# Filter layers and spectra at later positions, and one pool of twelve weight slots

## The chip, the cores and the metric

The kernel runs on one core of a Trainium2 chip, in one launch. The metric is the device time in microseconds; the figure for a kernel is the median of its runs. All times inside the kernel are from one profiled execution, counted from the start of its span.

## The reference, cut to what matters

Two blocks work on 256 tokens of width 1024, all in fp32. Each has a mixer, a layer norm, a mixture of experts and a layer norm. Block 0's mixer is an attention (with 256 context tokens), block 1's is a Hyena mixer, whose long filters don't depend on the tokens:

```
hid  = sin(sf[0] * (z @ w_in + b[0]))         # z: 256 x 33, constant
hid  = sin(sf[1] * (hid @ w_hid[0] + b[1]))   # 64 wide
hid  = sin(sf[2] * (hid @ w_hid[1] + b[2]))
filt = (hid @ w_out) * decay                  # 256 x 2 x 2 x 1024
spec = rfft(concat(fwd, 0, flip(bwd[1:])))    # per order o and channel
z    = gate * (irfft(rfft(z) * spec[o]) + z * skip[o])      # for o in 0, 1
# mixture of experts, 16 experts of 1024 x 1024 x 3, each token goes to two
ys   = (silu(x @ w_gate[e]) * (x @ w_up[e])) @ w_down[e]
```

Modulation vectors (`c @ mod_w`, 2 x 6 x 1024) scale and shift what goes into the mixers and experts.

## The kernel before, in words

**Stages.** Up to about 265 us: the attention, with the modulation vectors woven between its units. Then the output projection, the router and layer 0's experts (277 to 776), the Hyena mixer (788 to 907), its output projection and router, and layer 1's experts (957 to 1304), then the last layer norm.

**The ring.** All large weights go through tiles of 128 x 2048 fp32 (1 MB each), loaded by SP's queue in the order of the program as the scheduler fixes it (`load`, L146). There are RING = 12 slots, and during the experts of layer l MORE[l] = 4 or 5 further ones in a pool of their own. Before, each slot is a pool tag of its own with one buffer, and `turns` keeps the order in which they come up: a load waits until the one slot whose turn it is has been read out by its last user.

**Experts in positions.** `moe` (L730) takes an expert at a position p. Each needs 8 tiles for gate and up (L648), then 4 for down (L667); the tokens are picked by a one-hot matmul (`pick`, L616), turned (L628), and added back to `xs` (`back`, L686, L692). Positions 0 to 9 are always run. The two fullest experts are done densely for all tokens beside positions 1 to 8 (`PIECES`): at odd positions half of gate and up with 4 more tiles (`dense_up`, L711, L713), at even ones half of down with 2 more (`dense_down`, L723). So an odd position loads 16 tiles and an even one 14.

Positions 10 to 13 are rare: nested branches (`rare`, L761) run an expert only where tokens are left for it. In this data three run in layer 0 and none in layer 1 (108 loads each of gate, up and down tiles, four to an expert, are 27 experts: 12 in each layer and three). The branch is taken at position 9 (NEST), ahead of that position's own expert. Before the branch the queue loads 8 of position 9's tiles; inside it the rare experts use the other slots; after it come the 4 down tiles. What is loaded into a slot that the branch uses waits until TensorE has left the branch.

**Filters.** Layer 0's experts have a filler: `filler(p, bank)` is called at each position after the dense piece and ahead of `turn_in` and `down`. At position 0 it runs `filt_mlp` (loads on POOL's queue, then three layers, each a matmul L1172, six DVE steps L1174 to L1180, and a Sin on ScalarE L1182, each waiting for the one before) and the first two of eight spectra (`filt_spec`: matmuls L1212 and L1221, DVE steps L1213 and L1224, a store to DRAM L1225). FILL names the position of each spectrum. `spec_loads` for the next one (L1195 to L1200, on POOL's queue, one buffer) follows each.

**Hyena mixer.** Its input weights come as two raw tiles per section s of six; in sections 1 to 5 ScalarE and DVE split each into a high and a low part (L154, L155), which takes four more slots (`win_loads`). The spectra are read back into two slots per order (`spec_load`). NAHEAD = 4 raw tiles are asked for at the end of layer 0's experts.

Of the kernel before, what the change touches and what calls it, by code (L numbers as in the profile page):

```python
# [7 lines left out]
F32 = mybir.dt.float32  # L8
# [3 lines left out]
AF = mybir.ActivationFunctionType  # L12
# [14 lines left out]
RING = 12  # L27
# [10 lines left out]

PIECES = {1 + i: (i // 4, i // 2 % 2, i % 2) for i in range(4 * DENSE)}

FILL = [0, 0, 4, 6, 8, 8, 9, 9]

MODS = (12, 34)
MLAG = 2
# [31 lines left out]
def emit(tc, I, O):  # L76
# [3 lines left out]

    with es:
        cp = es.enter_context(tc.tile_pool(name="cp", bufs=1))
        ring = es.enter_context(tc.tile_pool(name="ring", bufs=1))
        accp = es.enter_context(tc.tile_pool(name="accp", bufs=1, space=PSUM))
        miscp = es.enter_context(tc.tile_pool(name="miscp", bufs=1, space=PSUM))
        dram = es.enter_context(tc.tile_pool(name="dram", bufs=1, space=DRAM))
# [15 lines left out]
                mturn[0] ^= 1  # L102
            return miscp.tile([128, 512], F32, name=f"mis{i}", tag=f"mis{i}")

        slots = {"order": list(range(RING)), "at": 0}

        def wtile(i=None):

            if i is None:
                i = turns()[0]  # L110
                slots["at"] += 1
            return (ring if i < RING else slots["pool"]).tile([128, 2048], F32, name=f"w{i}", tag=f"w{i}")

        def turns(order=None):

            if order is None:
                a = slots["at"] % len(slots["order"])
                return slots["order"][a:] + slots["order"][:a]
            slots["order"], slots["at"] = order, 0

        def more_ring(l):

# [4 lines left out]
            return xp, pool_  # L127

        def all_slots(n):
            turns(turns() + [RING + i for i in range(n)])  # L130

        def less_ring(pool_):
            turns([i for i in turns() if i < RING])
            for p_ in pool_:
                p_.__exit__(None, None, None)

# [437 lines left out]
        def expert_loads(l, idx, have=(), most=12, new=False):  # L574

            def src(nm, i):
                return expert_of(l, nm, idx)[256 * i:256 * i + 256, :].rearrange("(k p) f -> p k f", p=128)

            order = [(nm, i) for i in range(4) for nm in ("exp_w_gate", "exp_w_up")] + [("exp_w_down", i) for i in range(4)]
            ts = list(have)  # L580
            for nm, i in order[len(ts):]:
                ts.append(load(src(nm, i), [2, 1024], slot=RING + len(ts) if new else None))
                if len(ts) == most:
                    break
            return ts
# [144 lines left out]
        def moe(l, h2, R, first, filler):  # L730
            with tc.tile_pool(name=f"mp{l}", bufs=2, reuse_waits="tile") as mp:
# [73 lines left out]
                for p in range(RARE):  # L805
                    if p == NEST:

                        ix = number(1, place(p), [ET.SP], NE - 1)
                        w = expert_loads(l, ix, most=8)
                        last.back()  # L810
                        last = None
                        free = turns()
                        own, free = free[-8:], free[:-8]
                        turns(free)
                        rare(RARE)
                        E.bank = E.banks()
                        free.sort(key=lambda i: i < RING)
                        turns(free[:4])
                        E.w = expert_loads(l, ix, have=w)
                        turns(free[4:] + own + free[:4])  # L820
                    elif p == 0:
                        E.w = first
                    else:
                        ix = number(1, place(p), [ET.SP], NE - 1) if p > 1 else 1
                        E.w = expert_loads(l, ix, have=second if p == 1 else (), most=8)
                        if p in PIECES:
                            r, half, down = PIECES[p]
                            dw = dense_loads(l, number(1, 2 + r, [ET.SP], NE - 1), half, down)
                        E.w = expert_loads(l, ix, have=E.w)
                    E.up()  # L830
                    if last:
                        last.back()
                    nxt = expert(p + 1) if p + 1 < RARE else None
                    if nxt:
                        nxt.pick()
                    if p == 0:
                        for t in range(2):
                            dve.tensor_tensor(out=xs[:, t, :], in0=h2[:, t, :], in1=lng, op=ALU.mult)
                            for hf in range(2):
                                s_ = slice(512 * hf, 512 * hf + 512)  # L840
                                dve.tensor_tensor(out=xs[:, t, s_], in0=xs[:, t, s_], in1=lnb[hf], op=ALU.add)
                    E.turn_mid()
                    if p in PIECES:
                        if down:
                            dense_down(mp, E.bank, dw, hid[r], R["wtP"][:, :, 2 + r:3 + r], g2b)
                        else:
                            hid[r] = dense_up(mp, E.bank, dw, h2T)
                    if filler:
                        filler(p, E.bank)
                    if nxt:  # L850
                        nxt.turn_in()
                    if p != NEST:
                        E.weights_in()
                    E.down()
                    if p + 1 == NEST:
                        nxt.weights_in()
                    E, last = nxt, E
# [290 lines left out]
        spec = dram.tile([2, 4, 128, D], F32, name="spec")  # L1148
        fl_state = {}

        def filt_mlp():
            hft = fp.tile([128, 4, FQ], F32, name="hft", tag="stg")
            hfi = hft[0:33, 0, 0:64]
            pool.dma_start(out=hfi, in_=I["hy_ffn_w_in"][0])
            hfh = hft[0:64, 1, 0:128].rearrange("k (a m) -> k a m", a=2)
            pool.dma_start(out=hfh, in_=I["hy_ffn_w_hid"][0].rearrange("a k m -> k a m"))
            hfb = fp.tile([64, 6], F32, name="hfb")
            pool.dma_start(out=hfb[:, 0:3], in_=I["hy_ffn_b"][0].rearrange("a k -> k a"))
            pool.dma_start(out=hfb[:, 3:6], in_=I["hy_sin_freq"][0].rearrange("a k -> k a"))
            mt = fp.tile([128, 4, N], F32, name="mt", tag="PM")  # L1160
            zT = mt[0:33, 0]
            pool.dma_start(out=zT, in_=I["cst_z"])
            fl_state["FF"] = FF = fp.tile([128, 4, 128], F32, name="FF")
            pool.dma_start(out=FF, in_=I["cst_fw"].rearrange("p (c f) -> p c f", c=4))

            hs = fp.tile([128, 2, N], F32, name="hs")
            hid = zT
            kdim = 33
            for a in range(3):
                b = mbank()  # L1170
                w = hfi if a == 0 else hfh[:, a - 1, :]
                pe.matmul(b[0:64, 0:N], w, hid[0:kdim, :], start=True, stop=True)  # L1172
                u, k = mt[0:64, 1], mt[0:64, 2]
                dve.tensor_scalar(out=u, in0=b[0:64, 0:N], scalar1=hfb[:, a:a + 1], scalar2=hfb[:, 3 + a:4 + a],  # L1174
                                  op0=ALU.add, op1=ALU.mult)
                dve.tensor_scalar(out=k, in0=u, scalar1=1.0 / (2 * math.pi), scalar2=MAGIC, op0=ALU.mult, op1=ALU.add)
                dve.tensor_scalar(out=k, in0=k, scalar1=MAGIC, scalar2=None, op0=ALU.subtract)
                dve.scalar_tensor_tensor(out=u, in0=k, scalar=-C_HI, in1=u, op0=ALU.mult, op1=ALU.add)
                dve.scalar_tensor_tensor(out=u, in0=k, scalar=-C_LO, in1=u, op0=ALU.mult, op1=ALU.add)
                dve.tensor_scalar(out=u, in0=u, scalar1=PI_F, scalar2=-PI_F, op0=ALU.min, op1=ALU.max)  # L1180
                h = hs[0:64, 0, :] if a == 2 else mt[0:64, 3 if a == 0 else 0]
                act.activation(h, u, AF.Sin)  # L1182
                hid, kdim = h, 64
            dve.tensor_copy(hs[0:64, 1, :], hs[0:64, 0, :])
            dve.tensor_copy(hs[64:128, 0, :], hs[0:64, 0, :])
            dve.tensor_scalar(out=hs[64:128, 1, :], in0=hs[0:64, 0, :], scalar1=-1.0, scalar2=None, op0=ALU.mult)
            dve.memset(hs[64:128, :, 0:1], 0.0)
            fl_state["hs"] = hs

        def spec_loads(o, q):  # L1190
            c0 = FQ * q
# [35 lines left out]
        oq = [(o, q) for q in range(D // FQ) for o in range(2)]  # L1227

        def filler(p, bank):
            if p == 0:  # L1230
                filt_mlp()
                spec_loads(*oq[0])
            for i in [i for i, p_ in enumerate(FILL) if p_ == p]:
                filt_spec(*oq[i], bank)
                if i + 1 < len(oq):
                    spec_loads(*oq[i + 1])

        def win_tile(s, i):
            return load(wi[512 * i:512 * i + 512, 512 * s:512 * s + 512].rearrange("(k p) n -> p k n", p=128), [4, 512])

        with tc.tile_pool(name="fp", bufs=1, reuse_waits="tile", side="right") as fp:
            wi = I["hy_w_in"][0]
            moe(0, h2, R, first, filler)
            ws0 = [win_tile(j // 2, j % 2) for j in range(NAHEAD)]
        less_ring(rmore)

        R = routing_tables()
# [227 lines left out]
```

## Time and profile before

| | |
|---|---|
| median of 3 runs | 1320.58 us (1314.1 to 1323.14) |
| profiled execution | 1321.82 us, span 1320.1 us |
| granted TensorE clock, mean | 0.946 |
| TensorE busy | 1177.6 us (89%) |
| DVE busy | 550.0 us (42%) |
| ScalarE busy | 216.6 us (16%) |
| POOL busy | 48.4 us (4%) |
| moved by DMA | 443.88 MB, mean 336 GB/s, 426.76 MB of it on SP's queue |

The profiled execution is 1.2 us longer than the median. No engine is busy for the whole span and the transfers are not either: the stages differ, so that one has to look which of them has a hole where. The weights alone, 426.76 MB at some 408 GB/s, are over 1,040 us of transfers.

### The profile page before, as it was taken

The numbers are of one execution on the slowest core, as the hardware profiler recorded it, in microseconds if no ns is written. First come the engines' busy times: TensorE is split into PE (matmuls) and PEld (weight loads), VectorE is DVE, ScalarE is ACT, GpSimd is POOL, SyncE is SP. The second block draws the span as 40 slices with busy tenths as digits, with TensorE's granted clock in tenths as the row PEclk, the third lists the DMA queues.
The fourth block names the chain that finished last, engine by engine and source line by source line (L and its number), as shares of the span: only waits on it lengthen the run. The fifth ranks groups of instructions, "written<-read, shape, count | busy, mean of one in ns | idle before, by whom it ended". The sixth has DMA issues, their size and how long they took to land. (4 is left out here: it accounts for less than half of the span.)

```text
span 1320.1 us, 19948 instructions
## 1 busy us (share of the span) xinstructions
PE 1177.6 (89%) x8106; PEld 700.8 (53%) x8106; DVE 550.0 (42%) x1131; ACT 216.6 (16%) x431; POOL 48.4 (4%) x88
## 2 busy tenths in 40 slices
PE   5999989978999999999776779899799999999994
PEld 2444545434845648466432348675366465574842
DVE  2467998374122141321421157995530312313033
ACT  2133546130000000000000025321210000000000
POOL 1000000211000000000100010000100000000000
PEclk9999998978999999999977789899799999999998
DMA  9978986869599799999999794368499999999994
GB/s 329 397 287 318 336 328 234 319 260 394 217 405 405 267 397 405 408 398 392 398 395 409 275 372 159 127 225 334 180 393 408 401 390 359 402 374 402 408 383 160
DMA packets 133207, 443.88 MB, mean 336 GB/s; under 512 B 8271, under 2 KB 9895, under 8 KB 133104
## 3 DMA queue, kind: packets, MB, share of 16 engines
q1 hardware_dynamic: 127168, 426.76, 83.7%
q0 software_dynamic: 4864, 13.18, 2.9%
q10 hardware_dynamic: 1072, 2.54, 0.6%
q8 instruction: 68, 1.11, 0.3%
q14 instruction: 35, 0.29, 0.1%
HBM read 437.19 MB, written 5.26 MB: 335 GB/s over the span
## 5 line engine op out<-in xcount | busy, mean ns | idle before, releaser
L648 PE MATMUL acc<-w,xe 128*32 128x256 f32 (+1 forms) x2688 | 216.7, 428 | 17.9 <-PEq L761 7.4
L711 PE MATMUL acc<-xnT,w 128*128 128x256 f32 x1024 | 222.8, 379 | 0.4 <-DVE xs L692 0.4
L711 PEld LDWEIGHTS acc<-xnT,w 128*128 128x128 f32 x1024 | 194.3, 190 | 26.7 <-DVE xs L692 0.6
L648 PEld LDWEIGHTS acc<-w,xe 128*32 128x32 f32 (+1 forms) x2688 | 102.6, 120 | 121.4 <-issue 68.1
L667 PE MATMUL acc<-w,aT 128*32 128x256 f32 (+1 forms) x1344 | 120.2, 426 | 9.7 <-DMA w<-in_exp_w_down 3.9
L723 PE MATMUL acc<-w,hid 128*128 128x512 f32 x256 | 111.5, 593 | 0.3 <-DVE xs L692 0.3
L714 DVE TENSOR_TENSOR hid<-hid,acc 128x256 f32<-128x256 f32 x32 | 13.4, 420 | 190.4 <-ACT hid L713 190.4
L271 DVE SCALAR_TENSOR_TENSOR w<-w,cz,w 128x1024 f32<-128x1024 f32 x60 | 75.0, 1277 | 22.7 <-DMA w<-in_mod_w 22.6
L667 PEld LDWEIGHTS acc<-w,aT 128*32 128x32 f32 (+1 forms) x1344 | 48.4, 117 | 66.9 <-issue 30.0
L723 PEld LDWEIGHTS acc<-w,hid 128*128 128x128 f32 x256 | 48.0, 190 | 58.6 <-issue 57.6
L692 DVE TENSOR_TENSOR xs<-xs,acc 128x512 f32<-128x512 f32 x92 | 57.6, 683 | 47.1 <-PE acc L686 47.1
L652 DVE TENSOR_TENSOR ac<-ac,acc 128x256 f32<-128x256 f32 (+1 forms) x23 | 10.7, 467 | 148.3 <-PE acc L648 148.3
L943 PE MATMUL acc<-w,hT 128*128 128x512 f32 (+1 forms) x192 | 71.5, 523 | 0.9 <-DVE mr L166 0.8
L1296 PE MATMUL acc<-hTh,w 128*128 128x256 f32 x320 | 63.0, 293 | 5.4 <-DVE w L155 3.7
L1296 PEld LDWEIGHTS acc<-hTh,w 128*128 128x128 f32 x320 | 50.2, 190 | 9.7 <-DVE w L155 4.4
L725 DVE SCALAR_TENSOR_TENSOR do<-acc,wtP,g2b 128x512 f32<-128x512 f32 x32 | 24.0, 751 | 69.7 <-PE acc L723 69.7
L943 PEld LDWEIGHTS acc<-w,hT 128*128 128x128 f32 x192 | 35.4, 190 | 32.4 <-issue 29.2
L651 ACT ACTIVATE ac<-acc 128x256 f32<-128x256 f32 (+1 forms) x23 | 9.7, 420 | 254.9 <-PE acc L648 254.9
L616 PE MATMUL mis<-h,Pu 128*32 128x256 f32 (+1 forms) x336 | 38.1, 470 | 13.8 <-DVE Pu L610 9.9
L686 PE MATMUL acc<-xg,PT 32*128 32x256 f32 (+1 forms) x336 | 41.2, 434 | 6.0 <-DVE xg L672 4.6
L713 ACT ACTIVATE hid<-acc 128x256 f32<-128x256 f32 x32 | 12.3, 383 | 208.7 <-PE acc L711 208.7
L1296 PE MATMUL acc<-hTl,w 128*128 128x256 f32 x160 | 45.1, 283 | 0.0
(351 smaller groups left out, 1272.9 us busy)
## 6 DMA issues: line engine op xcount, KB each, us to landing
w<-in_exp_w_up SPq DMA_DIRECT2D x108, 1024.0 KB, 17.8
w<-in_exp_w_gate SPq DMA_DIRECT2D x108, 1024.0 KB, 17.7
w<-in_exp_w_down SPq DMA_DIRECT2D x108, 1024.0 KB, 10.8
w<-in_mod_w SPq DMA_DIRECT2D x40, 1024.0 KB, 9.6
w<-in_hy_w_in SPq DMA_DIRECT2D x12, 1024.0 KB, 13.8
w<-in_attn_w_in SPq DMA_DIRECT2D x9, 1024.0 KB, 13.1
w<-in_mod_w SPq DMA_DIRECT2D x16, 512.0 KB, 10.8
w<-in_attn_w_out SPq DMA_DIRECT2D x4, 1024.0 KB, 13.4
```

The lines of the kernel that those rows point to most:

```text
L271: dve.scalar_tensor_tensor(out=st["acc"][:, k], in0=w[:, k], scalar=c_[k], in1=st["acc"][:, k], op0=ALU.mult, op1=ALU.add)
L616: pe.matmul(gb[S * j:S * j + S, 0:nn], Pu[:, t, 0:S], self.h2[:, t, nn * j:nn * j + nn], start=(t == 0), stop=(t == 1), tile_position=(0, ...
L648: pe.matmul(A[m][S * j:S * j + S, 0:nn], self.xe[:, kc, :], w[:, nn * j:nn * j + nn], tile_position=(0, S * j), start=(kc == 0), stop=(kc ...
L667: pe.matmul(y[S * q:S * q + S, 0:nn], lhs, w[:, nn * q:nn * q + nn], tile_position=(0, S * q), start=(kc == 0), stop=(kc == KC - 1))
L686: pe.matmul(o, self.PT[r, 128 * t:128 * t + 128], self.yb[r, 0:nn], start=True, stop=True, tile_position=(S * q, 0))
L692: dve.tensor_tensor(out=x_, in0=x_, in1=o, op=ALU.add)
L711: pe.matmul(b[:, N * m:N * m + N], ws[m][kc // 4][:, kc % 4, 128 * fb:128 * fb + 128], h2T[:, kc, :], start=(kc == 0), stop=(kc == KC - 1))
L714: dve.tensor_tensor(out=hid[:, fb, :], in0=hid[:, fb, :], in1=b[:, N:2 * N], op=ALU.mult)
L723: pe.matmul(b, hid[:, fb, 128 * t:128 * t + 128], ws[fb // 2][:, fb % 2, s_], start=(fb == 0), stop=(fb == 3))
L725: dve.scalar_tensor_tensor(out=o, in0=b, scalar=wt[:, t], in1=g2b[:, s_], op0=ALU.mult, op1=ALU.mult)
L943: pe.matmul(bank[:, 0:width], hT[:, kc, 128 * t:128 * t + 128], st["w"][kc // per][:, kc % per, :], start=(kc == 0), stop=(kc == KC - 1))
L1296: pe.matmul(b[:, 0:N], w_, m, start=(kc == 0 and i == 0), stop=(kc == KC - 1 and i == len(ps) - 1))
```

## The change

The first layer of the MLP goes to position 1, the second to 2, the third, with the loads for the first spectrum, to 3. The spectra go from positions 0, 0, 4, 6, 8, 8, 9, 9 to 4, 6, 7, 8, 8, 8, 9, 9. The twelve ring slots become one tag with twelve buffers, so that the pool hands out a slot; only the further ones are still named. At position 8 the further slots leave the turn ahead of its down loads. Position 9 loads 4 (layer 0) or 5 (layer 1) tiles into the further slots before the branch, in place of 8, and the other 8 or 7 into the ring after it; the rare experts have all twelve ring slots.

```
-FILL = [0, 0, 4, 6, 8, 8, 9, 9]
+FILL = [4, 6, 7, 8, 8, 8, 9, 9]
+FMLP = [1, 2, 3]
...
-        ring = es.enter_context(tc.tile_pool(name="ring", bufs=1))
+        ring = es.enter_context(tc.tile_pool(name="ring", bufs=RING))
...
-        slots = {"order": list(range(RING)), "at": 0}
+        slots = {"turn": RING - 1, "more": 0}
         def wtile(i=None):
             if i is None:
-                i = turns()[0]
-                slots["at"] += 1
-            return (ring if i < RING else slots["pool"]).tile([128, 2048], F32, name=f"w{i}", tag=f"w{i}")
+                slots["turn"] = (slots["turn"] + 1) % (RING + slots["more"])
+                i = slots["turn"] - RING
+            if i < 0:
+                return ring.tile([128, 2048], F32, name="w", tag="w")
+            return slots["pool"].tile([128, 2048], F32, name=f"w{i}", tag=f"w{i}")
...
         def all_slots(n):
-            turns(turns() + [RING + i for i in range(n)])
+            slots["more"] = n
+            slots["turn"] = RING + n - 1
...
                     if p == NEST:
                         ix = number(1, place(p), [ET.SP], NE - 1)
-                        w = expert_loads(l, ix, most=8)
+                        w = expert_loads(l, ix, most=MORE[l], new=True)
                         last.back()
                         last = None
-                        free = turns()
-                        own, free = free[-8:], free[:-8]
-                        turns(free)
                         rare(RARE)
                         E.bank = E.banks()
-                        free.sort(key=lambda i: i < RING)
-                        turns(free[:4])
                         E.w = expert_loads(l, ix, have=w)
-                        turns(free[4:] + own + free[:4])
...
+                        if p + 1 == NEST:
+                            all_slots(0)
                         E.w = expert_loads(l, ix, have=E.w)
...
         def filler(p, bank):
-            if p == 0:
-                filt_mlp()
-                spec_loads(*oq[0])
+            for i in [i for i, p_ in enumerate(FMLP) if p_ == p]:
+                filt_mlp(i)
+                if i == 2:
+                    spec_loads(*oq[0])
             for i in [i for i, p_ in enumerate(FILL) if p_ == p]:
                 filt_spec(*oq[i], bank)
                 if i + 1 < len(oq):
                     spec_loads(*oq[i + 1])
...
-            ws0 = [win_tile(j // 2, j % 2) for j in range(NAHEAD)]
+            ws0 = [win_tile(j // 2, j % 2, -1) for j in range(NAHEAD)]
```

The body of `filt_mlp` is split into `filt_load` (all its loads, called with layer 0) and one layer per call, with the same instructions.

## Rows read from the trace of the kernel before

**Rows 1.** The page's slices, 33 us each: granted clock and transfers, in tenths.
```profile
PEclk9999998978999999999977789899799999999998
DMA  9978986869599799999999794368499999999994
```

**Rows 2.** Windows of layer 0: busy us (instructions) by engine, clock, transfers, GB/s.
```profile
281.00:318.00 37.00, 31.37 (x358) 16.29 (x350) 22.61 (x57) 4.83 (x10) 4.62 (x8) 0.97 0.99 379
318.00:330.30 12.30, 10.82 (x29) 4.35 (x27) 4.65 (x11) 0.93 (x3) 0.80 (x1) 0.61 1.03 395
338.50:353.50 15.00, 15.00 (x71) 13.22 (x70) 0.96 (x3) 0.77 (x2) 0.00 (x0) 1.00 0.06 25
433.00:441.50 8.50, 8.50 (x42) 7.47 (x41) 0.84 (x2) 0.60 (x2) 0.00 (x0) 1.00 0.02 9
448.00:603.00 155.00, 151.91 (x1241) 95.14 (x1234) 44.91 (x96) 9.20 (x24) 5.43 (x9) 1.00 1.03 402
664.70:742.00 77.30, 54.13 (x638) 25.23 (x638) 11.06 (x27) 3.06 (x8) 0.00 (x0) 0.76 0.99 394
742.00:751.00 9.00, 4.34 (x48) 2.09 (x52) 2.90 (x5) 0.00 (x0) 0.00 (x0) 0.69 0.09 20
```

**Rows 3.** SP's queue in order of time, position 1: start, us, what was issued.
```profile
353.31 3.83 SPq L146 DMA_DIRECT2D w<-in_exp_w_down  x3
```

**Rows 4.** SP's queue, layer 1's position 9: last load before the branch, first four behind.
```profile
1268.23 2.16 SPq L146 DMA_DIRECT2D w<-in_exp_w_up  x1
1289.06 3.27 SPq L146 DMA_DIRECT2D w<-in_exp_w_down  x4
```

**Rows 5.** Windows of layer 1, around the branch.
```profile
1220.00:1280.00 60.00, 58.22 (x424) 39.62 (x416) 11.61 (x22) 3.45 (x9) 0.00 (x0) 1.00 1.02 408
1284.00:1291.00 7.00, 2.80 (x44) 1.89 (x44) 2.91 (x5) 0.00 (x0) 0.00 (x0) 0.94 0.29 83
1291.00:1303.50 12.50, 10.49 (x165) 6.37 (x161) 0.42 (x1) 2.05 (x3) 0.00 (x0) 0.90 0.83 328
```

**Rows 6.** Groups of instructions in 285 to 319: busy us, mean ns, idle before.
```profile
L667 PE MATMUL acc<-w,aT 128*32 128x256 f32 x64 | 4.5, 382 | 0.5 <-ACT aT L164 0.5
L1221 PE MATMUL acc<-PM,FF 128*128 128x256 f32 x16 | 4.3, 398 | 0.0
L1212 PE MATMUL acc<-fwo,hs 128*128 128x256 f32 x16 | 4.2, 396 | 3.2 <-DMA fwo<-in_hy_ffn_w_out 2.7 <-issue 0.4
L1172 PE MATMUL mis<-mt,hft 64*64 64x256 f32 (+1 forms) x6 | 1.9, 402 | 0.2 <-ACT mt L1182 0.2
```

**Rows 7.** TensorE in order of time, layer 0's position 9 [idle before, releaser].
```profile
749.66 9.36 PE L648 MATMUL acc<-w,xe 128*32 128x256 f32 x128 [3.73 <-PEq L761]
...
767.61 3.48 PE L1212 MATMUL acc<-fwo,hs 128*128 128x256 f32 x8 [3.11 <-DMA fwo<-in_hy_ffn_w_out]
...
774.40 1.93 PE L667 MATMUL acc<-w,aT 128*32 128x256 f32 x30
```

**Rows 8.** TensorE in order of time, the second spectrum at position 8.
```profile
647.67 3.02 PE L1212 MATMUL acc<-fwo,hs 128*128 128x256 f32 x8 [3.78 <-DMA fwo<-in_hy_ffn_w_out]
650.62 1.65 PE L667 MATMUL acc<-w,aT 128*32 128x256 f32 x16
652.21 1.99 PE L1221 MATMUL acc<-PM,FF 128*128 128x256 f32 x8
```

**Rows 9.** TensorE, a block of 16 down matmuls at either clock.
```profile
711.62 1.87 PE L667 MATMUL acc<-w,aT 128*32 128x256 f32 x16 [0.61 <-DMA w<-in_exp_w_down]
...
1303.43 1.07 PE L667 MATMUL acc<-w,aT 128*32 128x256 f32 x16 [0.86 <-DMA w<-in_exp_w_down]
```

**Rows 10.** Waits in the attention and the Hyena stage: us in total, times, longest.
```profile
DVE w L271 <- DMA w<-in_mod_w: 22.6, 4, 11.4
...
ACT w L154 <- DVE ed L1335: 11.5, 2, 7.1
ACT w L154 <- DMA w<-in_hy_w_in: 9.4, 3, 4.7
```

**Rows 11.** SP's queue in the Hyena stage.
```profile
774.76 1.15 SPq L146 DMA_DIRECT2D w<-in_hy_w_in  x2
...
813.86 0.92 SPq L146 DMA_DIRECT2D w<-in_hy_w_in  x2
```

More of the change, by code (lines that the diff above doesn't have):

```diff
@@ L103, in mbank @@
             return miscp.tile([128, 512], F32, name=f"mis{i}", tag=f"mis{i}")
-        slots = {"order": list(range(RING)), "at": 0}
+        slots = {"turn": RING - 1, "more": 0}
         def wtile(i=None):
             if i is None:
-                i = turns()[0]
-                slots["at"] += 1
-            return (ring if i < RING else slots["pool"]).tile([128, 2048], F32, name=f"w{i}", tag=f"w{i}")
[L114 to L119, printed above, removed]
+                slots["turn"] = (slots["turn"] + 1) % (RING + slots["more"])
[3 more added lines that the diff above has]
+            return slots["pool"].tile([128, 2048], F32, name=f"w{i}", tag=f"w{i}")
         def more_ring(l):
@@ L129, in all_slots @@
         def all_slots(n):
-            turns(turns() + [RING + i for i in range(n)])
+            slots["more"] = n
+            slots["turn"] = RING + n - 1
         def less_ring(pool_):
-            turns([i for i in turns() if i < RING])
+            all_slots(0)
             for p_ in pool_:
@@ L581, in expert_loads @@
             for nm, i in order[len(ts):]:
-                ts.append(load(src(nm, i), [2, 1024], slot=RING + len(ts) if new else None))
+                ts.append(load(src(nm, i), [2, 1024], slot=len(ts) if new else None))
                 if len(ts) == most:
@@ L828, in moe @@
                             dw = dense_loads(l, number(1, 2 + r, [ET.SP], NE - 1), half, down)
+                        if p + 1 == NEST:
+                            all_slots(0)
                         E.w = expert_loads(l, ix, have=E.w)
@@ L1149, in emit, with filt_load @@
         fl_state = {}
-        def filt_mlp():
+        def filt_load():
             hft = fp.tile([128, 4, FQ], F32, name="hft", tag="stg")
@@ L1160, in filt_mlp @@
             mt = fp.tile([128, 4, N], F32, name="mt", tag="PM")
-            zT = mt[0:33, 0]
-            pool.dma_start(out=zT, in_=I["cst_z"])
+            pool.dma_start(out=mt[0:33, 0], in_=I["cst_z"])
             fl_state["FF"] = FF = fp.tile([128, 4, 128], F32, name="FF")
             pool.dma_start(out=FF, in_=I["cst_fw"].rearrange("p (c f) -> p c f", c=4))
[L1166 to L1188, printed above, removed]
+            fl_state["hs"] = fp.tile([128, 2, N], F32, name="hs")
+            fl_state["mlp"] = hfi, hfh, hfb, mt, mt[0:33, 0], 33
+        def filt_mlp(a):
+            if a == 0:
+                filt_load()
+            hs = fl_state["hs"]
+            hfi, hfh, hfb, mt, hid, kdim = fl_state["mlp"]
+            b = mbank()
+            w = hfi if a == 0 else hfh[:, a - 1, :]
+            pe.matmul(b[0:64, 0:N], w, hid[0:kdim, :], start=True, stop=True)
+            u, k = mt[0:64, 1], mt[0:64, 2]
+            dve.tensor_scalar(out=u, in0=b[0:64, 0:N], scalar1=hfb[:, a:a + 1], scalar2=hfb[:, 3 + a:4 + a],
+                              op0=ALU.add, op1=ALU.mult)
+            dve.tensor_scalar(out=k, in0=u, scalar1=1.0 / (2 * math.pi), scalar2=MAGIC, op0=ALU.mult, op1=ALU.add)
+            dve.tensor_scalar(out=k, in0=k, scalar1=MAGIC, scalar2=None, op0=ALU.subtract)
+            dve.scalar_tensor_tensor(out=u, in0=k, scalar=-C_HI, in1=u, op0=ALU.mult, op1=ALU.add)
+            dve.scalar_tensor_tensor(out=u, in0=k, scalar=-C_LO, in1=u, op0=ALU.mult, op1=ALU.add)
+            dve.tensor_scalar(out=u, in0=u, scalar1=PI_F, scalar2=-PI_F, op0=ALU.min, op1=ALU.max)
+            h = hs[0:64, 0, :] if a == 2 else mt[0:64, 3 if a == 0 else 0]
+            act.activation(h, u, AF.Sin)
+            fl_state["mlp"] = hfi, hfh, hfb, mt, h, 64
+            if a == 2:
+                dve.tensor_copy(hs[0:64, 1, :], hs[0:64, 0, :])
+                dve.tensor_copy(hs[64:128, 0, :], hs[0:64, 0, :])
+                dve.tensor_scalar(out=hs[64:128, 1, :], in0=hs[0:64, 0, :], scalar1=-1.0, scalar2=None, op0=ALU.mult)
+                dve.memset(hs[64:128, :, 0:1], 0.0)
@@ L1236, in filler, with win_tile @@
                     spec_loads(*oq[i + 1])
-        def win_tile(s, i):
-            return load(wi[512 * i:512 * i + 512, 512 * s:512 * s + 512].rearrange("(k p) n -> p k n", p=128), [4, 512])
+        def win_tile(s, i, slot=None):
+            return load(wi[512 * i:512 * i + 512, 512 * s:512 * s + 512].rearrange("(k p) n -> p k n", p=128), [4, 512], slot=slot)
         with tc.tile_pool(name="fp", bufs=1, reuse_waits="tile", side="right") as fp:
```

## The prediction

> **What bounds the kernel now.** I read the slices first: the DMA row says which stages wait for weights, the clock row where TensorE was kept busy [rows 1]. In layer 0's experts (277 to 776 us) and layer 1's (957 to 1304) the DMA row is near full except for a few holes, so there a hole is time lost unless the engine behind it is the slow one. The windows name the holes. At 338.5 to 353.5 the transfers run at 0.06 while TensorE is busy for all 15.00 us, and at 433 to 441.5 at 0.02 while TensorE is busy for all 8.50 [rows 2]: the ring is full and waits for position 1's and position 3's dense matmuls, and the SP queue shows the first load after the stop at 353.31 [rows 3]. From 448 to 603 both are full: TensorE 151.91 of 155.00 us, transfers 1.03 [rows 2]. In the rare experts it is the transfers alone: 0.99 against TensorE's 54.13 of 77.30, and then they stop (0.09 in 742 to 751) until the branch is behind TensorE [rows 2]. So TensorE sets the pace from position 0 to about 8, and the weights after that.
>
> In layer 1 no rare expert runs. TensorE is busy 58.22 of 60.00 us up to 1280, and after the empty branch the queue issues position 9's last four loads at 1289.06 [rows 4, 5]. The chain of waits ends on the last of these.
>
> **Position 0 is cleared.** The MLP and two spectra there keep TensorE for 1.9 + 4.2 + 4.3 = 10.4 us and make it wait for DVE, ScalarE and one filter load [rows 6]. From the MLP's first matmul (290.9) to the dense matmuls of position 1 (330.3) pass 39.4 us. What is left without them is position 0's down (4.5, [rows 6]), position 1's up (its 128 matmuls are the 9.36 us of [rows 7]) and what fills 318 to 330.3, the back, position 2's pick and the transposes: 10.82 us at a granted clock of 0.61, so 6.6 at full [rows 2]. With some 3 us of hand-overs that is 23.5. I take -16. Bounds: -10.4, the busy time alone, and -18. The transfers allow it: they are full in 281 to 318, and position 1's twelve outstanding loads, 2.57 us each (1,024 KB at the 408 GB/s of [rows 5]), are there by some 313. As TensorE bounds what follows, its shift carries: the 15 us hole shrinks to some 3, and the hole at 433 stays, 16 us sooner.
>
> **What is put back on that path.** Three MLP steps: one matmul pair each, 1.9 / 3 = 0.6, so +1.9 in all; their DVE chain lies beside dense matmuls, where DVE has 44.91 of 155 us to do, and the next step is a position later. If that cover is gone each chain costs what it did at position 0, some 3 us. The spectrum at position 7 costs its matmuls, (4.3 + 4.2) / 2 = 4.2, its filter loaded long before. Position 8 gets a third. A second one in the same position shows the price: TensorE waits 3.78 for the filter, then 3.02 and 1.99 of matmuls [rows 8]: 8.8, less the little down work that slips between, say 8.5. Bounds 4.2 (wait filled) to 10. In sum +14.6, so the first rare expert starts only 1.4 us sooner. Their POOL loads stand in POOL's own queue with nothing else behind them. Position 8's down loads may now use the twelve slots alone, and wait until position 7's down gives two back: a hole of some 7 us in the transfers, hidden because position 8's down is not due for 25 us and the ring is full again before the rare experts.
>
> **The rare experts.** Before, 4 + 12 + 12 loads were outstanding when the first rare expert began (28 at 2.57 us); after, with all twelve slots, its own twelve are there and 24 remain: -10.3. Bounds: 0 if the ring makes the queue wait between experts, -13 if it also hides part of the third spectrum. The end of the branch comes 11.7 us sooner.
>
> **Position 9, layer 0.** Eight loads instead of four stand behind the branch, because every ring slot was last used inside it. The last lands 10.3 us later after the branch. But the two spectra hold position 9 until 776.4 anyway: the second waits 3.11 us for its filter and the last down matmuls follow it at 774.40, while the four loads were there by about 763 [rows 7], if they took the 14.3 us from issue to the last landing that layer 1 shows (1289.06 to 1303.4, [rows 4]). What is late next is the up, whose second half needs four of the new loads (5 to 6 us), and part of that is filled by the first spectrum. I take +3, bounds -2 and +10.3. Layer 0 in sum: -16 + 14.6 - 10.3 + 3 = -8.7.
>
> **Position 9, layer 1.** No spectra, no rare expert: five loads before, seven behind instead of four. TensorE passes the branch when it did, as position 8 bounds it, so three more loads lie bare: 3 x 2.57 = +7.7, bounds +5 and +10. The hole before the branch (0.29 in 1284 to 1291, [rows 5]) only grows.
>
> With TensorE waiting on each load its clock falls: the last 16 down matmuls took 1.87 us in the rare stage against 1.07 at layer 1's end [rows 9]. The Trainium skill says the same (TensorE: Matmul & The Clock Gate, "What's actually happening"): an array left idle drops to half its clock and has to be kept busy to get it back. By that rule both positions 9 would pay some 0.8 us more and the result would be 1.6 higher; the row decides nothing here, since 1291 to 1303.5 already held waits.
>
> **The pool of slots.** No row shows how a pool orders its slots. A slot held long no longer blocks the load whose turn it is. The nearest rows for a gain: DVE waits 22.6 us for modulation weights, 11.4 of them at the start where no slot matters, and in the Hyena stage ScalarE's split copies wait 11.5 and 9.4 us [rows 10]. DVE and TensorE are both near full there, so few of these 32 us reach the end. A loss is as possible: the queue ran loads out of order before, and a pool may hand out slots in program order. Bounds -20 and +24 (below). I take -4, nearer the small waits than the sum.
>
> **Sum.** -8.7 + 7.7 - 4 = -5.0. The profiled execution took 1321.8 us, 1.2 above the median of the runs shown: 1316.8 by it, **1315.6** against the median.
>
> **Rivals.** (1) The pool pays, and TensorE's start in position 1 is as early as its upper bound: -12 for the pool, -18 at position 0, 2 more from position 9: about 1302 (1290 to 1307). For it: the waits of [rows 10]; against: full engines beside them. Chance 0.27.
> (2) Slower, by one mechanism: slots handed out in program order in the Hyena stage. Each section's raw weights would be asked for only after the section before has taken its split tiles. Now section 2's go out at 774.76, sections later at 813.86 [rows 11], and splits begin at 791.6. If they wait for the splits, each of the four pairs lands some 6 us after it is due: +24, about 1340 (1334 to 1346). It decides from some 18 us. For it: ScalarE waited for these loads already; against: slots come back earlier too. Chance 0.18.
> (3) The gain of position 0 is eaten: third spectrum at 10, position 9 at +10, the rare stage no shorter; layer 1's loss stays: -16 + 16 + 10 + 7.7 - 4 = +13.7 at its worst, some +8 as a rule: 1329 (1324 to 1334). Chance 0.13.
> The forecast (1307 to 1324, with 0.08 of its chance just below) has 0.42; that the pool changes nothing, the slots coming back in the old turn, is inside it: 1319.6.
>
> **Chances.** A measurement tells 1% (13.2 us) from no change, so faster is below 1307.4 and slower above 1333.8. Faster 0.27 + 0.08 = 0.35; slower 0.18; same 0.34 + 0.13 = 0.47. The range, 1296 to 1339, leaves out 0.08 at the end of (1) and 0.12 of (2).
>
> **What would show it.** Position 0 right: position 1's dense matmuls begin near 314 and the hole at 338.5 is 3 us, not 15. Put back: the first rare expert's up near 663. Rare stage: transfers stop near 730. Layer 1: seven loads issued together at the branch, and 20 us from there to the last down matmul instead of 15. Wrong if the attention or Hyena stage moves by more than 10 us, if position 8 waits for its down loads, or if the loads behind the branch are issued before TensorE passes it.

## The result: 1.3% faster, more than three times the forecast gain

The changed kernel takes 1301.18 us (median of 4 runs, 1297.5 to 1304.26) beside 1317.44 for the kernel before on the same chip: ratio 0.9867, 95% interval 0.9839 to 0.9895, so 17.5 us less (13.8 to 21.2; 16.3 by the two medians). The forecast was -5. The two traces lie further apart, by 24.4 us of span: the changed kernel's profile is of its fastest run, as is that of the first experiment's kernel, and the one before lies 4.4 us above its kernel's median. So the shares below are also taken from kernels with one part of the change alone.

**Where the time came from.** Start times of the same work in five traces, in us; a number with a sign is the shift against the trace before. The kernel of the first experiment has the new pool and position 9, that of the second the new filter positions alone, that of the third the new position 9 alone.

```
                               before    after   1st     2nd     3rd
layer 0, position 0's up        278.2    -7.8    -6.9    +0.3    -0.3
position 1's dense matmuls      330.4   -34.7   -11.6   -26.6    -0.5
position 3's dense matmuls      418.8   -33.5   -12.0   -25.4    -0.4
position 5's dense matmuls      498.8   -26.7   -12.0   -18.6    -0.4
position 7's dense matmuls      580.9   -30.2   -12.0   -22.1    -0.4
position 8's dense matmuls      624.0   -26.8   -12.0   -18.7    -0.4
first rare expert's up          664.7   -18.7   -12.1   -10.2    -0.6
position 9's up, behind branch  749.7   -29.6   -21.7    -9.9   -10.4
Hyena stage's first transpose   784.2   -27.0   -18.6    -9.5    -7.0
layer 1, position 1's dense     979.9   -32.4   -24.0   -11.3    -5.5
layer 1, position 7's dense    1223.4   -32.3   -24.0   -11.3    -5.5
end of the span                1320.1   -24.4   -14.1   -10.3    +2.6
```

The changed kernel's slices, for [rows 1]:

```profile
PEclk9999999989999999999778789999899999999986
DMA  9999894879998998999999784378799999999964
```

Against [rows 1] the third DMA digit, 66 to 99 us, is 9 instead of 7: the attention stage's transfers are held up less there. The drop from 9 to 6 at the end is layer 1's position 9. Windows of the changed kernel, for [rows 2, 5] (columns as there):

```profile
280.00:295.70 15.70, 14.83 (x225) 8.28 (x226) 6.01 (x17) 1.07 (x4) 0.00 (x0) 1.00 1.04 395
...
318.00:330.00 12.00, 12.00 (x106) 7.89 (x106) 2.14 (x4) 0.38 (x1) 0.00 (x0) 1.00 1.03 410
...
400.00:410.00 10.00, 10.00 (x48) 8.83 (x47) 0.55 (x2) 0.38 (x1) 0.00 (x0) 1.00 0.55 209
410.00:445.00 35.00, 35.00 (x236) 16.44 (x235) 11.11 (x21) 1.53 (x4) 0.00 (x0) 1.00 1.02 398
445.00:472.00 27.00, 23.53 (x289) 12.10 (x288) 15.65 (x43) 2.34 (x6) 2.35 (x4) 1.00 1.04 394
...
490.00:498.00 8.00, 8.00 (x39) 7.07 (x38) 0.42 (x1) 0.38 (x1) 0.00 (x0) 1.00 0.32 104
...
712.00:716.00 4.00, 2.88 (x28) 0.98 (x24) 0.42 (x1) 0.00 (x0) 0.00 (x0) 0.50 0.04 15
...
1250.00:1260.00 10.00, 5.92 (x80) 3.19 (x76) 2.90 (x5) 0.00 (x0) 0.00 (x0) 0.80 0.23 69
```

Position 0's down, position 1's up and what follows them lie in 15.7 us at a clock of 1.00; the 15 us hole of [rows 2] at 338.5 is gone, and the one at 433 has become a half hole in 400 to 410. From 410 to 488 the transfers are full, and in 445 to 472 TensorE is idle for 3.5 of 27.00 us. It does not wait for weights there; these are all its waits:

```profile
PE mis L614 <- DVE PT L164: 2.1, 2, 1.5
PE acc L655 <- DVE ac L650: 0.6, 1, 0.6
PE mis L626 <- ACT xg L162: 0.6, 1, 0.6
```

They are hand-overs from DVE and ScalarE, most of them around the pick for the next experts. In 490 to 498 the transfers stop again while TensorE is busy for all 8.00 us: SP's queue waits up to 17.6 us for position 5's dense matmuls (L709), so TensorE still sets the pace. Transfers stop at 712 before the branch, not at 742. The waits for modulation and Hyena weights that [rows 10] shows are nearly gone. DVE's in the changed kernel, the whole of them at the start, where no slot matters:

```profile
DVE w L269 <- DMA w<-in_mod_w: 11.4, 1, 11.4
```

ScalarE's, in the Hyena stage:

```profile
ACT w L152 <- DMA w<-in_hy_w_in: 4.5, 1, 4.5
```

Layer 1's position 9 on SP's queue, for [rows 4]:

```profile
1231.65 0.37 SPq L144 DMA_DIRECT2D w<-in_exp_w_gate  x1
1256.60 0.39 SPq L144 DMA_DIRECT2D w<-in_exp_w_up  x1
1257.32 0.37 SPq L144 DMA_DIRECT2D w<-in_exp_w_gate  x1
1257.95 0.76 SPq L144 DMA_DIRECT2D w<-in_exp_w_up  x1
1258.92 2.08 SPq L144 DMA_DIRECT2D w<-in_exp_w_down  x4
```

Five loads are out by 1231.65, seven follow together at 1256.60. From there to the end of the last down matmul pass 23.6 us (1280.17); before, 15.4 (1289.06 to 1304.50, [rows 4, 9]).

### The profile page after: what moved, and what is told of

Its sections match the earlier page's. It is cut to its first block, busy times and chain, and to the rows that moved or that the text cites. A ratio compares the mean times of both kernels' runs of the same rounds, so it can differ in the third digit from the quotient of the medians.

```text
span 1295.7 us, 19951 instructions
## 1 busy us (share of the span) xinstructions
PE 1161.9 (90%) x8106; PEld 696.2 (54%) x8106; DVE 549.3 (42%) x1131; ACT 214.9 (17%) x431; POOL 48.8 (4%) x88
## 5 line engine op out<-in xcount | busy, mean ns | idle before, releaser
L709 PE MATMUL acc<-xnT,w 128*128 128x256 f32 x1024 | 222.3, 379 | 0.0
L709 PEld LDWEIGHTS acc<-xnT,w 128*128 128x128 f32 x1024 | 194.4, 190 | 25.6
L665 PE MATMUL acc<-w,aT 128*32 128x256 f32 (+1 forms) x1344 | 115.5, 420 | 10.2 <-DMA w<-in_exp_w_down 6.0
L269 DVE SCALAR_TENSOR_TENSOR w<-w,cz 128x1024 f32<-128x1024 f32 x60 | 75.8, 1289 | 11.4 <-DMA w<-in_mod_w 11.4
L1294 PE MATMUL acc<-hTh,w 128*128 128x256 f32 x320 | 59.9, 286 | 0.0
L614 PE MATMUL mis<-h,Pu 128*32 128x256 f32 (+1 forms) x336 | 33.6, 462 | 13.3 <-DVE Pu L608 8.5
## 6 DMA issues: line engine op xcount, KB each, us to landing
w<-in_exp_w_gate SPq DMA_DIRECT2D x108, 1024.0 KB, 17.5
```

The source lines that it names most:

```text
L269: dve.scalar_tensor_tensor(out=st["acc"][:, k], in0=w[:, k], scalar=c_[k], in1=st["acc"][:, k], op0=ALU.mult, op1=ALU.add)
L614: pe.matmul(gb[S * j:S * j + S, 0:nn], Pu[:, t, 0:S], self.h2[:, t, nn * j:nn * j + nn], start=(t == 0), stop=(t == 1), tile_position=(0, ...
L665: pe.matmul(y[S * q:S * q + S, 0:nn], lhs, w[:, nn * q:nn * q + nn], tile_position=(0, S * q), start=(kc == 0), stop=(kc == KC - 1))
L709: pe.matmul(b[:, N * m:N * m + N], ws[m][kc // 4][:, kc % 4, 128 * fb:128 * fb + 128], h2T[:, kc, :], start=(kc == 0), stop=(kc == KC - 1))
L1294: pe.matmul(b[:, 0:N], w_, m, start=(kc == 0 and i == 0), stop=(kc == KC - 1 and i == len(ps) - 1))
```

## The experiments

Each ratio is to the kernel before on the same chip (its median there 1320 to 1321 us).

**1. Pool and position 9, filters back where they were.**
```
-FILL = [4, 6, 7, 8, 8, 8, 9, 9];  FMLP = [1, 2, 3]
+FILL = [0, 0, 4, 6, 8, 8, 9, 9];  FMLP = [0, 0, 0]
```


> The changed kernel with the filters' work back where it was (three inner layers and two spectra at position 0, the third of position 8 gone): what is left of the change is the pool of twelve and position 9's loads. Theory A, the parts add: the pool is worth 7.8 us in the attention stage and 5.4 us in the Hyena stage, the loads of position 9 give 10.9 - 2.5 in layer 0 and take 7.9 in layer 1, so 13.6 us below the kernel before, about 1304. Position 0's up starts near 270.4, position 1's dense matmuls some 7 to 8 us before 330.35, as the filters' work at position 0 is back. Theory B, the earlier start in the attention stage is swallowed at position 0 and the pool gains nothing without it: 1317, no difference.


Measured: 1311.48, ratio 0.9948 (0.9925 to 0.9971). Theory A in its places: -6.9 in the attention stage, and a trace 14.1 shorter. By the ratio it is 6.9 us (3.8 to 9.9), half of A's 13.6, and the interval holds neither that nor B's nothing.

**2. The filters alone, in the kernel before.**
```
-FILL = [0, 0, 4, 6, 8, 8, 9, 9]     (inner layers and first loads at position 0)
+FILL = [4, 6, 7, 8, 8, 8, 9, 9];  FMLP = [1, 2, 3]
```


> The kernel before with the filters' work alone moved as in the change (inner layers one at each of positions 1, 2 and 3; spectra at 4, 6, 7, 8, 8, 8, 9, 9); slots in the old turn and position 9 as before. Theory A, the parts add: position 0 loses some 19 us (39.4 to about 20 from the old first inner layer to position 1's dense matmuls), 8 of them are lost again where the transfers bind between positions 3 and 5, 3.4 go to the spectrum at position 7 and 8 to the third at position 8 less what gives way there; the first rare expert starts 11 us before 664.7 and the end comes 11 us sooner, about 1306. Theory B, as predicted: 1.4 us sooner, about 1316. Theory C, the gain at position 0 needs the pool's loads to be there: 1317 or more.


Measured: 1309.03, ratio 0.9923 (0.9902 to 0.9944), 10.2 us less. Theory A by its size; B (-1.4) is outside the interval. A's reason for the loss between positions 3 and 5, transfers that bind there, is not borne out (see "Put back" below). TensorE in order of time in this kernel (start, us, ...):

```profile
290.04 3.66 PE L669 MATMUL acc<-w,aT 128*32 128x256 f32 x64 [0.47 <-ACT aT L166]
293.52 7.09 PE L650 MATMUL acc<-w,xe 128*32 128x256 f32 x128
300.54 1.15 PE L688 MATMUL acc<-xg,PT 32*128 32x256 f32 x16
301.61 1.94 PE L618 MATMUL mis<-h,Pu 128*64 128x512 f32 x8
303.48 0.44 PE L659 MATMUL acc<-blob,ac 128*128 128x128 f32 x2
303.76 1.46 PE L713 MATMUL acc<-xnT,w 128*128 128x256 f32 x6
```

Down, up, back, pick and transposes follow each other without a gap. The kernel before did the last steps like this:

```profile
317.97 1.13 PE L686 MATMUL acc<-xg,PT 32*128 32x256 f32 x6
320.57 1.86 PE L686 MATMUL acc<-xg,PT 32*128 32x256 f32 x6 [1.48 <-DVE stg L1224]
322.36 1.97 PE L616 MATMUL mis<-h,Pu 128*64 128x512 f32 x2
324.26 2.07 PE L686 MATMUL acc<-xg,PT 32*128 32x256 f32 x4
326.26 3.68 PE L616 MATMUL mis<-h,Pu 128*64 128x512 f32 x6
```

The same 16 back and 8 pick matmuls lie over 12 us there instead of 3: they stand behind the second spectrum's evacuation (stg), and that waited on ScalarE until the first spectrum was stored:

```profile
318.92 0.66 ACT L164 ACTIVATE stg<-acc 128x256 f32<-128x256 f32 x2 [2.94 <-DMA spec<-stg]
```

From 322 to 330 the granted clock is 0.50 (1.2 GHz instead of 2.4). Two pick matmuls that need 0.5 us in the second kernel, so 1.0 at that clock, show as 1.97 "busy".

**3. Position 9's loads alone, in the kernel before.**
```
-w = expert_loads(l, ix, most=8)          own, free = free[-8:], free[:-8]
+w = expert_loads(l, ix, most=MORE[l])    own, free = free[-MORE[l]:], free[:-MORE[l]]
```


> The kernel before with position 9's loads alone changed: four of them (five in layer 1) issued ahead of the branch in place of eight, the rest behind it, and twelve slots instead of eight or nine left to the rare experts; filters and turn as before. Theory A: the rare experts end 10.3 to 10.9 us sooner, position 9 of layer 0 takes 2.5 to 3 longer, position 9 of layer 1 takes 7.7 to 7.9 longer: in sum within 1 us of the kernel before, 1317, with the shifts to be read at the branch of each layer. Theory B, the rare stage got shorter by the pool's order and not by the number of slots: nothing won in layer 0, +10 in all, about 1328.


Measured: 1325.18, ratio 1.0038 (1.0015 to 1.0062), 5 us more where 0 was expected. The trace has A's terms: rare experts -9.8, layer 0's position 9 +3.4, layer 1's +8.1; the Hyena stage took 1.5 more. B is out, since the rare stage gained with the old turn. By itself this part does not pay.

**The pool by difference.** The first kernel less the third is the pool, with the further slots kept for position 9's early loads: -11.9 us by the ratios, -16.7 by the spans: 6.6 in the attention stage, 4.5 at position 0, 0.5 from there to the Hyena stage, 6.9 in it, less 1.8 at the end. The 4.5 lie in position 0's last steps: back and pick take 6.0 us in the first kernel (from 312.4 on, at a clock of 1.00), 12 in the kernel before. That the pool causes this is not shown. SP's queue in the Hyena stage of the first kernel, with the pool (start, us, what was issued):

```profile
757.02 38.03 SPq L144 DMA_DIRECT2D w<-in_hy_w_in  x4
801.39 9.13 SPq L144 DMA_DIRECT2D w<-spec  x2
810.61 25.13 SPq L144 DMA_DIRECT2D w<-in_hy_w_in  x4
```

And of the third kernel, with the turn:

```profile
768.53 7.67 SPq L146 DMA_DIRECT2D w<-in_hy_w_in  x2
797.81 4.28 SPq L146 DMA_DIRECT2D w<-spec  x2
810.00 38.13 SPq L146 DMA_DIRECT2D w<-in_hy_w_in  x6
```

Counted from each stage's first transpose (765.6 and 777.2), the last section load is out at 70 us with the pool and at 71 with the turn. But of the four section loads that stand first here, the third and fourth are out by 29 us with the pool, and not before 33 with the turn, which lets only two go ahead of the second spectra. These times do not explain the gain: in the kernel before, too, the turn lets only two go ahead, but the third and fourth are out by 29.7 us ([rows 11], from 784.2), the last by 67.8, and its stage is still 5.4 us longer than the changed kernel's. What differs is the waits of ScalarE's split copies. The third kernel has these, close to [rows 10]; the first has none of the first kind and one of 4.6 us of the second:

```profile
ACT w L154 <- DVE ed L1335: 11.4, 2, 7.0
ACT w L154 <- DMA w<-in_hy_w_in: 10.9, 4, 4.7
```

The first line names the slot. DVE's L1335 (`ed<-ed,w`) multiplies with a spectrum, read from its ring tile, and the split copy cannot write its part before that: the slot whose turn it was still held a spectrum.

**4. A spectrum moved from position 8 to 5.**
```
-FILL = [4, 6, 7, 8, 8, 8, 9, 9]
+FILL = [4, 5, 6, 7, 8, 8, 9, 9]
```


> The changed kernel with the spectra at positions 4, 5, 6, 7, 8, 8, 9, 9: one of position 8's three moved to position 5, where TensorE was seen to wait for transfers (7.3 us of 10 busy in 460 to 470). Theory A: position 5 takes it in its waits at no cost and position 8 is rid of its 8.1 us, so 6 to 8 us below the changed kernel, about 1294, all of it by the first rare expert (646 to 639). Theory B, a spectrum costs its 4.2 us of matmuls wherever it stands and only the wait for its filter is saved: 4 us, about 1297. Theory C, the transfers bind up to position 8 and the time is lost again there: 1301, no difference.


Measured: 1298.46, ratio 0.9856 (0.9816 to 0.9897): the changed kernel's, though B's 1297 is inside the interval too. Counted from position 0's up, it is 4.7 us later at position 7's dense matmuls (0.6 of it from ahead of the spectrum, 4.1 the spectrum's: B, as it came behind the dense matmuls), 3.6 ahead at the first rare expert, and 0.6 ahead behind the branch: its rare stage took 77.1 us, not 74.1. So C at the end by the trace: the transfers stop 441 us after position 0's up in both kernels, and what TensorE gains ahead of the rare experts is waited for again. The idle time that A meant to fill is hand-overs, as shown above, not waits for transfers.

**5 and 6. Accumulators released two steps sooner, in the kernel before and in the changed one.**
```
-RLAG = 3
+RLAG = 1
```


> The kernel before with RLAG 1 instead of 3: a vector's first modulation tile, which is its accumulator and stays in its slot over four steps and the lag, is read out by TensorE two steps sooner, and its slot is free two steps sooner. Theory A, the fixed turn waited at the accumulators' slots in the attention stage: a part of the 6.6 us that the pool gained there comes without the pool; layer 0's first up starts 2 to 6 us before 278.2, and the rest of the kernel is shifted by that, 1315 to 1319. Theory B, the turn's waits are at other slots (attention weights, split tiles): the first up stays within 1 us of 278.2. Theory C, TensorE waits for the sums when they are asked for that soon: later than 278.2.


Measured: 1317.34, ratio 0.9978 (0.9958 to 0.9998); the first up at 274.9, 3.3 us sooner. Theory A: half of the pool's gain in this stage comes without the pool. But the third DMA digit stays at 7. In 66 to 99 us the queue of the kernel before waits for slots that matmuls on attention weights read, and these two waits are the same in this one, which adds 7.2 us for an accumulator's (L283):

```profile
SPq L146 <- PE acc L943: 13.8, 2, 9.8
SPq L146 <- PE acc L1088: 8.8, 1, 8.8
```

So B's reason, other slots, holds for a part of the stage.

> The changed kernel with RLAG 1 instead of 3. Theory A, a pool that hands out what is free goes around a held accumulator, so that its length of stay matters little: the first up within 1.5 us of 270.4, no difference to the changed kernel, about 1301. Theory B, the pool too stops at a held slot: 2 to 6 us sooner, 1296 to 1299. Theory C, TensorE waits for the sums: later.


Measured: 1301.06, ratio 0.9853 (0.9815 to 0.9892); the first up at 272.9. The interval holds both A's 1301 and B's 1296 to 1299; the first up, which is no sooner, speaks for A. It is later than 270.4: the eight kernels with the pool put it at 270.4 to 272.9, so the changed kernel's trace is at the early end; the three with the old turn and lag have 277.9 to 278.5.

**7. The branch behind position 9, in layer 1.**
```
-if p == NEST:          (loads, rare(RARE), the other loads)
+if p == NESTS[l]:      with NESTS = [9, -1]
...
 last.back()
+if l: all_slots(0); rare(RARE)
```


> The changed kernel with the branch on further rare experts behind position 9 in layer 1 (it is not taken there with these data), so that all twelve loads of position 9 follow position 8's without a stop. Theory A, the seven loads behind the branch are what position 9 waits for: TensorE's up starts near 1253 at full pace (7.1 us, 9.2 before), the last back near 1267 instead of 1280.7, and the branch costs some 4 us at the end unhidden: 9 to 14 us below the changed kernel, about 1289. Theory B, the branch costs at the end what it cost ahead of position 9, and the loads were hidden but for three: 4 us, about 1297. Theory C, transfers bind at the end of layer 1 whether a branch stands there or not: 1301.


Measured: 1288.63, ratio 0.9778 (0.9742 to 0.9815), some 12 us below the changed kernel: Theory A. TensorE's position 9 in layer 1 there:

```profile
1256.66 6.25 PE L647 MATMUL acc<-w,xe 128*32 128x256 f32 x112
1263.53 0.44 PE L656 MATMUL acc<-blob,ac 128*128 128x128 f32 x2 [0.61 <-DVE ac L651]
1264.50 2.80 PE L666 MATMUL acc<-w,aT 128*32 128x256 f32 x48 [0.53 <-ACT aT L163]
1267.58 1.07 PE L666 MATMUL acc<-w,aT 128*32 128x256 f32 x16 [0.28 <-SPq L760]
1269.20 1.15 PE L685 MATMUL acc<-xg,PT 32*128 32x256 f32 x16 [0.55 <-DVE xg L671]
```

And in the changed kernel:

```profile
1256.92 9.18 PE L646 MATMUL acc<-w,xe 128*32 128x256 f32 x112 [3.53 <-PEq L759]
...
1273.25 1.93 PE L665 MATMUL acc<-w,aT 128*32 128x256 f32 x16 [2.04 <-DMA w<-in_exp_w_down]
1275.80 1.94 PE L665 MATMUL acc<-w,aT 128*32 128x256 f32 x16 [0.62 <-DMA w<-in_exp_w_down]
1278.31 1.86 PE L665 MATMUL acc<-w,aT 128*32 128x256 f32 x16 [0.57 <-DMA w<-in_exp_w_down]
1280.73 1.15 PE L684 MATMUL acc<-xg,PT 32*128 32x256 f32 x16 [0.56 <-DVE xg L670]
```

The waits for loads and for the branch (PEq) are gone but for 0.28 us, and 16 down matmuls take 1.07 us instead of 1.9. From the last back to the end pass 15.4 us against 15.0: at the end the branch costs some 0.4.

**8. The same in both layers.**
```
-NESTS = [9, -1]
+NESTS = [-1, -1]
```


> As the kernel with the branch behind position 9 in layer 1, and the same in layer 0, where rare experts do run. Theory A: position 9 of layer 0 then has all its loads in the stream and its two spectra lie beside transfers, but the rare experts end the layer and the Hyena stage's first weights are asked for behind the branch: 5 to 8 us gained on loads, 4 to 8 lost at the Hyena stage's start, so within 4 us of the kernel with layer 1's alone, about 1289. Theory B, the rare stage is bound by transfers that now never stop: 8 us better, 1281. Theory C, position 9 was the cover of the spectra's filter loads and of the Hyena weights' start, which now lie bare: 10 us worse, 1299.


Measured: 1285.17, ratio 0.9736 (0.9701 to 0.9772), which overlaps the seventh's: between A and B, not told apart. In this kernel TensorE waits 2.48 us for the Hyena stage's first weights.

**9. The inner layers back at position 0.**
```
-FMLP = [1, 2, 3]
+FMLP = [0, 0, 0]
```


> The changed kernel with the three inner layers back at position 0 (spectra as in the change). Theory A, past position 3 the transfers bind and not TensorE: position 1's dense matmuls start 4 to 6 us later against position 0's up (25.3 us from the up to the dense matmuls in the changed kernel), the difference is gone by position 5's dense matmuls as less time is lost to the transfers there (18.6 of 26.6 us was kept), and the time is within 2 us of the changed kernel, 1301. Theory B, time at position 0 is carried to the end, as the prediction had it: 4 to 6 us at position 5 and at the end, 1306. Theory C, the inner layers are what made position 0 long (their chain of DVE and ScalarE), not the spectra: more than 12 us at position 1.


Measured: 1306.16, ratio 0.9915 (0.9881 to 0.9949). From position 0's up to position 1's dense matmuls 30.2 us, to position 5's 203.9; in the changed kernel 25.3 and 201.7. So 4.9 at position 1, of which 2.2 are left at position 5. That is not transfers taking it back, as A has it: 1.9 of the 2.7 that go are the three inner layers' own matmuls, which the changed kernel does in between. At the first rare expert it is 3.9, and the time is B's; A's 1301 is outside the interval, which just overlaps the changed kernel's. C is out: of the 22.1 us that the position is shorter with the pool (47.4 in the first kernel) the spectra are 17.2.

**10. The eighth and the fourth together.**
```
-FILL = [4, 6, 7, 8, 8, 8, 9, 9]     (with NESTS = [-1, -1])
+FILL = [4, 5, 6, 7, 8, 8, 9, 9]
```


> The kernel with the branch behind position 9 in both layers, and the spectra at 4, 5, 6, 7, 8, 8, 9, 9. Theory A, transfers bind from position 8 to the end of layer 0: what TensorE gains at position 8 (3.6 us) is waited for again, 1285, no difference. Theory B, with no stop in the transfers ahead of the branch the 3 us that were lost in the rare stage are kept: 1282.


Measured: 1284.26, ratio 0.9746 (0.9713 to 0.9778): no difference to the eighth, as A has it; B's 1282 is just inside the interval, and in the trace 1.7 us are kept at the Hyena stage's first transpose (counted from position 0's up). The seventh, the eighth and this one beat both kernels of the case.

## Why the prediction was half right

The time, 1301.2, is inside the range, but outside the forecast's own part of it (1307 to 1324): it is the first rival's (1302). That is luck in part. The rival's terms add to 1303.6; its 12 us for the pool came by the ratios, but position 0 gave 26.6 for its 18, and its 2 more from position 9 did not come. Term by term, from the kernels with one part:

```
                                  forecast   measured
position 0 cleared                  -16       -26.6   (2nd)
put back, up to the rare experts    +14.6     +16.4   (2nd)
rare experts                        -10.3      -9.8   (3rd; after -10.9)
position 9, layer 0                  +3        +3.4   (3rd; after +2.6)
position 9, layer 1                  +7.7      +8.1   (3rd; after +7.9)
pool                                 -4       -16.7   (1st less 3rd; -11.9 by ratios)
```

The right column adds to -25.2, where the two traces are 24.4 us apart and the ratio gives -17.5: so a term from single traces can be off by some us.

**Position 0: the step that failed** is "what is left without them", put at 23.5 us. It was 12.6 (291.2 to 303.8 in the second kernel). Each piece was taken from a row in which TensorE was not at its own pace: the down at 4.5 [rows 6], in three parts with MLP matmuls between, for 3.66; the 128 up matmuls at 9.36 [rows 7], at a granted clock of 0.75, for 7.09; the stretch from 318 on at 6.6, scaled by the clock [rows 2], for 3.5; and 3 us of hand-overs that aren't there. These make 9.2 of the 10.9 us; the rest is that the down starts 1.2 earlier, and overlap. Scaling by the clock would have been right for the up (9.36 x 0.75 = 7.0), but it does not remove what counts as busy while a matmul is held up: the 1.97 us above are twice what the clock explains. The kernel before shows both steps undisturbed at other positions:

```profile
456.30 7.11 PE L648 MATMUL acc<-w,xe 128*32 128x256 f32 x128
608.63 3.66 PE L667 MATMUL acc<-w,aT 128*32 128x256 f32 x64
```

The result is beyond the bound of -18 that was given.

**Put back: right but for 2.7 us of waits.** The third spectrum cost 8.5 as forecast (the second kernel's shift goes from -18.7 at position 8's dense matmuls to -10.2 at the first rare expert), the one at position 7 3.4 for 4.2, the inner layers some 0.6 each, 1.9, as forecast. Between positions 3 and 5 the shift falls by 6.8, and 3.5 come back by position 7. Windows from one position's dense matmuls to the next's, 3 to 5 and 5 to 7, first the kernel before, then the changed one:

```profile
418.82:498.77 79.95, 79.56 (x599) 49.13 (x597) 21.76 (x47) 5.11 (x13) 2.39 (x4) 1.00 0.90 346
498.77:580.90 82.13, 79.43 (x674) 51.31 (x675) 25.08 (x55) 4.68 (x13) 3.04 (x5) 1.00 1.03 402
...
385.27:472.08 86.81, 83.34 (x638) 50.44 (x637) 29.33 (x70) 5.62 (x14) 2.35 (x4) 1.00 0.97 377
472.08:550.68 78.60, 76.25 (x638) 49.71 (x637) 20.73 (x42) 4.60 (x12) 3.08 (x5) 1.00 0.95 371
```

In the first stretch TensorE is busy 3.8 us longer: 0.6 for the third inner layer, 3.2 for work that changed places (64 pick matmuls for 32 there, 32 for 64 in the second, which is 3.2 shorter). Lost are 2.7 us of idle time (5.8 for 3.1 in both), the hand-overs shown above. 1.9 + 3.4 + 8.5 + 2.7 make the measured 16.4 but for 0.1. Why the picks moved ahead is not shown. "As TensorE bounds what follows, its shift carries" held; but the 15 us hole did not shrink to 3, it went, and half of the one at 433 went too. For position 8's down loads, where a hole of 7 us was forecast, the transfers lose 3.3 us (580 to 588, share 0.59), and TensorE waits for none of them.

**Rare experts and both positions 9** came as worked out from 2.57 us a load. That the half clock costs little there also held: the last block of 16 down matmuls took 1.86 us at a granted clock of 0.55, for 1.07 at 1.00 [rows 9], so 0.8 more; the earlier slow blocks lay beside loads. This agrees with the Trainium skill (TensorE: Matmul & The Clock Gate, "What's actually happening"), by which an idle array falls to half its clock.

**The pool: right sign, a third of the size.** The reason against it, full engines beside the waits of [rows 10], was wrong: of the 32 us of waits that a slot could shorten 27.6 are gone in the changed kernel, and with the pool the attention and the Hyena stage are 6.6 and 6.9 us shorter, where "few" were to reach the end; 4.5 more at position 0 were not foreseen at all. The fifth and sixth runs show one mechanism, a turn that stops at an accumulator's slot, for 3.3 us of the attention stage. That slots of attention weights and of spectra hold the rest is read from the waits; no run tests it. The second rival, slots in program order, did not come: four section loads are issued ahead of the second spectra, where the turn let two go. Of the third rival layer 1's loss is real, but not the rest of it.

**Stated signs.** Right: the hole at 338.5 shrinks, seven loads together at the branch, some 8 us more behind it, no wait of position 8 for its down loads. Wrong: position 1's dense matmuls at 295.7 for 314, the first rare expert at 646 for 663, the stop of the transfers at 712 for 730.

## What to carry to other kernels

To price work that stays, take its rows from a stretch where nothing holds the engine; elsewhere the busy time already has the wait in it. Before time is called lost between two points of a stretch, count the instructions between them: half of 6.8 us was work that had changed places. An engine that idles beside full transfers need not wait for them: look at what ends its waits. Loads for what follows a branch that is seldom taken belong ahead of it; where all cannot be held, move the branch.

## What was not expected

A spectrum at position 0 costs twice its matmuls (17.2 us for two that have 8.5 of them), at position 5 just its matmuls (4.1), at position 8 twice again (8.5), where it waits for its own filter load. An empty branch that cost 3.5 us of TensorE's time ahead of position 9, and kept seven loads behind it, cost some 0.4 at the end of the kernel.
